# Softmax over 16,384 rows: which rows a partition holds

## The chip, the core and the metric

The kernel runs on one core of a Trainium2 chip. The core has compute engines of its own: VectorE (DVE in the profile), ScalarE (ACT), GpSimd (POOL) and TensorE (PE, unused here), and SyncE (SP), which issues the transfers. They work on an on-chip memory of 128 partitions. Sixteen DMA engines move data between that memory and the DRAM. The metric is device time in microseconds (us), from the start of an execution to its end; less is better.

## The reference

The input `x` is float32 of shape 16 x 1024 x 512, so 16,384 rows of 512 numbers (2 KB each, 33.55 MB in all). Each row is replaced by its softmax, and no row needs another:

```python
x_max = np.max(x, axis=-1, keepdims=True)
exp_x = np.exp(x - x_max)
return exp_x / np.sum(exp_x, axis=-1, keepdims=True)
```

## The kernel before

Every partition handles 128 rows. They are worked on in 16 groups of `GROUP = 8` rows per partition, so one group is 128 x 8 = 1,024 rows, 2 MB. `LOADS` and `STORES` (lines 20 and 21) join two groups to a transfer: eight loads L0 to L7 and eight stores S0 to S7, each of 128 partitions x 16 rows x 2 KB = 4 MB.

The buffer `ring` (line 78) has room for `RING = 12` groups, so six of the eight loads fit. L6 takes the place of S0's data and must wait until S0 has been written out; L7 waits for S1 in the same way (`before`, line 97, and the waits at line 197).

What is done with one group:

- The maxima of its rows, negated, on VectorE (`rowmax`, line 145; two groups at once for the `MM` entries).
- `exp(x - max)` in place and the sum of each row, on ScalarE, one instruction per row of each partition (`exps`, line 134), in a loop over the 16 groups.
- The reciprocal of the sums on VectorE (line 159), and the product of the rows and the reciprocals (line 161), on VectorE for ten groups and on GpSimd for six.

Order and queues: `SEQUENCE` (line 31) is the order of the work on VectorE and GpSimd, written by hand. `ORDER` (line 26) is that of the transfers after the first six loads: S0 S1 L6 L7 S2 S3 S4 S5 S6 S7. All sixteen transfers are issued by SyncE, on one queue, in the order L0 to L5 and then `ORDER`. A store is issued when both of its groups have been scaled (line 170). The first load is moved ahead of the barrier at the start of the program (`loads_at_the_head`).

Which rows of the DRAM a transfer touches is decided by `in_dram` (line 117), for loads (line 127) and stores (line 131) alike. Before the change, the rows are cut into eight blocks of 2,048, one for each load; inside a block partition p holds the 16 rows from 16p on. A transfer therefore touches one block of 4 MB without a gap, and the piece of one partition begins 32 KB behind that of the partition before it.

Of the kernel before, what the change touches and what calls it, by code (L numbers as in the profile page):

```python
# [15 lines left out]
GROUP = 8  # L16
# [3 lines left out]
LOADS = [2, 2, 2, 2, 2, 2, 2, 2]  # L20
STORES = [2, 2, 2, 2, 2, 2, 2, 2]
GROUPS = sum(LOADS)
LOAD_AT = [sum(LOADS[:k]) for k in range(len(LOADS))]
# [37 lines left out]
def kernel(  # L61
# [7 lines left out]
    P = nc.NUM_PARTITIONS  # L69

    x_rows, out_rows = x.flatten_outer_dims(), out.flatten_outer_dims()
    d = x_rows.shape[1]
# [17 lines left out]
    def load_of(g):  # L90
        return max(k for k in range(len(LOADS)) if LOAD_AT[k] <= g)
# [23 lines left out]
        return t[:, at(g) * GROUP : (at(g) + groups) * GROUP]  # L115

    def in_dram(t, g, groups):
        k = load_of(g)
        assert load_of(g + groups - 1) == k
        part = t[P * GROUP * LOAD_AT[k] : P * GROUP * (LOAD_AT[k] + LOADS[k]), :]  # L120
        first = (g - LOAD_AT[k]) * GROUP
        part = part.rearrange("(p r) d -> p r d", p=P)
        return part[:, first : first + groups * GROUP, :]

    def load(k):
        g, n = LOAD_AT[k], LOADS[k]
        return nc.sync.dma_start(out=rows(g, n), in_=in_dram(x_rows, g, n))

    def store(k):
        g, n = STORE_AT[k], STORES[k]  # L130
        return nc.sync.dma_start(out=in_dram(out_rows, g, n), in_=rows(g, n))
# [42 lines left out]
    with tc.manual_schedule(engines={SP}):  # L174
        for k in range(min(before)):
            first = load(k).then_inc(loaded[k], 16)
# [6 lines left out]
    for work in SEQUENCE.split():  # L183
        kind = work.rstrip("0123456789")
        g = int(work[len(kind) :])
# [4 lines left out]
    for transfer in ORDER.split():  # L190
        k = int(transfer[1:])
# [39 lines left out]
```

## Time and profile before

| | |
|---|---|
| Median of 3 timed runs | 159.82 us (159.81 to 160.81) |
| The profiled execution: own time | 160.08 us |
| Its span, first to last recorded work | 158.8 us |
| VectorE busy | 121.8 us, 77% of the span, 36 instructions |
| ScalarE busy | 92.2 us, 58%, 257 instructions |
| GpSimd busy | 42.3 us, 27%, 10 instructions |
| Moved by the DMA engines | 67.11 MB in 2,304 packets, 423 GB/s over the span |
| A load, from issue to landing | median 25.9 us |
| A store, from issue to landing | median 24.0 us |

The own time is longer than the span by 1.28 us, which lie outside of the recorded work. The time of a transfer from issue to landing includes its wait in the queue behind earlier transfers, so it is not the time that moving 4 MB takes. Busy shares are averages: VectorE works from 12 us to 138 us and hardly pauses in between, while the DMA engines work from the first microsecond to the last.

### The profile page before, as it was taken

Reading aid. Unit: us, or ns where it says so; the run is one execution under the profiler, and the core shown is the slowest. Engines: PE = TensorE matmul, PEld = TensorE weight load, DVE = VectorE, ACT = ScalarE, POOL = GpSimd, SP = SyncE. Lnnn points to the kernel's source line nnn. Section 1 sums busy time; section 2 is a strip of 40 time slices with the busy share of each in tenths; the row PEclk is TensorE's granted clock in tenths of the full one; section 3 lists DMA queues with packets and bytes.
Section 4 is the critical chain, followed back from the end, with each engine's and each line's share of the span. In section 5 each row is a group of like instructions: output and inputs, shape, how many; then the busy total and the mean of one; then the engine's idle time right before and its main releaser. Section 6 shows DMA issues by size and latency. Waiting matters only on the chain.

```text
span 158.8 us, 572 instructions
## 1 busy us (share of the span) xinstructions
DVE 121.8 (77%) x36; ACT 92.2 (58%) x257; POOL 42.3 (27%) x10
## 2 busy tenths in 40 slices
DVE  0008979999999999999999499999999999700000
ACT  0300699969406999999988990899599300000000
POOL 0000000000007903930970790079049300000000
DMA  7999999999999999999999999999999999999996
GB/s 264 438 479 405 405 495 421 396 438 471 413 405 438 471 405 396 396 413 471 438 396 462 446 413 405 454 421 438 438 421 446 413 446 438 438 421 438 429 429 264
DMA packets 2304, 67.11 MB, mean 423 GB/s; under 512 B 256, under 2 KB 256, under 8 KB 256
## 3 DMA queue, kind: packets, MB, share of 16 engines
q1 hardware_dynamic: 2304, 67.11, 98.9%
HBM read 33.55 MB, written 33.55 MB: 423 GB/s over the span
## 4 chain that ended last, share of the span: by engine, by line
DMA 45%; DVE 39%; issue 2%; DVEq 0%
DMA ring<-in_x_dram 26%; DVE ring L161 22%; DMA out_dram<-ring 20%; DVE stat L145 16%; DVE recip L159 1%; DVEq L144 0%
## 5 line engine op out<-in xcount | busy, mean ns | idle before, releaser
L134 ACT ACTIVATE ring<-ring,stat x128 | 90.4, 707 | 28.1 <-ACTq L151 28.1
L145 DVE TENSOR_REDUCE stat<-ring 128x16 f32<-128x8192 f32 (+1 forms) x10 | 69.5, 6956 | 15.7 <-DMA ring<-in_x_dram 15.7
L161 POOL TENSOR_TENSOR ring<-ring,recip 128x4096 f32<-128x4096 f32 x6 | 42.1, 7016 | 81.8 <-DVE recip L159 81.8
L161 DVE TENSOR_TENSOR ring<-ring,recip 128x4096 f32<-128x4096 f32 x10 | 51.1, 5109 | 0.3
L134 ACT ACTIVATION_READ_ACCUMULATOR ring<-ring,stat x128 | 23.8, 186 | 0.0
L181 ACT ACT_TABLE_LOAD x1 | 1.3, 1283 | 4.0 <-PEq L179 4.0
L159 DVE RECIPROCAL recip<-stat 128x8 f32<-128x8 f32 x16 | 3.0, 190 | 0.0
L215 POOL MEMSET const-float32-0.0<- 128x1 f32 x1 | 0.1, 98 | 0.2 <-issue 0.2
L215 POOL MEMSET const-bfloat16-1.0<- 128x1 bf16 x1 | 0.1, 102 | 0.0
L215 POOL MEMSET const-uint8-127<- 128x1 uint8 x1 | 0.1, 102 | 0.0
L215 POOL MEMSET const-float32-1.0<- 128x1 f32 x1 | 0.1, 98 | 0.0
## 6 DMA issues: line engine op xcount, KB each, us to landing
ring<-in_x_dram SPq DMA_DIRECT2D x8, 4096.0 KB, 25.9
out_dram<-ring SPq DMA_DIRECT2D x8, 4096.0 KB, 24.0
```

The lines of the kernel that those rows point to most:

```text
L134: return nc.scalar.activation(out=row, in_=row, func=EXP, bias=one, scale=1.0, accum_out=one)
L145: nc.vector.reduce_max(out=cols(stat, g, groups), in_=rows(g, groups), axis=AX, negate=True).then_inc(maxima, groups)
L159: nc.vector.reciprocal(out=cols(recip, g), in_=cols(stat, g)).then_inc(inverted, 1)
L161: engine.tensor_mul(out=rows(g), in0=rows(g), in1=spread(cols(recip, g))).then_inc(scaled[store_of(g)], 1)
L181: nc.scalar.preload_act_table(EXP)
L215: nc = _bacc.Bacc("TRN2", target_bir_lowering=False, num_devices=1)
```

## The change

Only `in_dram` changes. The whole tensor is now split over the partitions at once: partition p holds the 128 rows from 128p on, one piece of 256 KB. Transfer k takes rows 16k to 16k + 15 of each partition's piece. A transfer still moves 128 pieces of 32 KB, but the pieces begin 256 KB apart in the DRAM, with gaps that the other seven transfers fill. Input and output are cut in the same way.

```diff
     def in_dram(t, g, groups):
-        k = load_of(g)
-        assert load_of(g + groups - 1) == k
-        part = t[P * GROUP * LOAD_AT[k] : P * GROUP * (LOAD_AT[k] + LOADS[k]), :]
-        first = (g - LOAD_AT[k]) * GROUP
-        part = part.rearrange("(p r) d -> p r d", p=P)
-        return part[:, first : first + groups * GROUP, :]
+        assert load_of(g + groups - 1) == load_of(g)
+        part = t.rearrange("(p r) d -> p r d", p=P)
+        return part[:, g * GROUP : (g + groups) * GROUP, :]
```

The buffers on the chip, the order of the sixteen transfers, the waits and every compute instruction are as before. In both built programs each transfer is one instruction over 128 x 8192 numbers; on the DRAM side the step from one partition to the next is 8,192 numbers before and 65,536 after, and the start of the second transfer is number 1,048,576 before and 8,192 after.

## The prediction

> **What bounds the kernel.** I first read the page's busy slices and its DMA lines, since the change touches nothing but transfers. The rows of digits are the busy tenths of 40 slices of the span (4 us each):
>
> ```profile
> DVE  0008979999999999999999499999999999700000
> ACT  0300699969406999999988990899599300000000
> ...
> DMA  7999999999999999999999999999999999999996
> ...
> DMA packets 2304, 67.11 MB, mean 423 GB/s; under 512 B 256, under 2 KB 256, under 8 KB 256
> ## 3 DMA queue, kind: packets, MB, share of 16 engines
> q1 hardware_dynamic: 2304, 67.11, 98.9%
> ```
>
> The DMA row has no gap from end to end, and packets occupy 98.9% of the sixteen engines' span. VectorE is nearly full in the middle but has nothing to do in the last five slices, which belong to stores alone. The packet line also tells the size of a piece: 256 of the 2,304 packets are tiny (16 transfers x 16 engines, the completion signals), so 2,048 carry data, 16 transfers x 128 partitions, and 67.11 MB / 2,048 is 32,768 bytes. One packet is already one partition's 16 rows.
>
> Then the chain that ended last:
>
> ```profile
> DMA 45%; DVE 39%; issue 2%; DVEq 0%
> DMA ring<-in_x_dram 26%; DVE ring L161 22%; DMA out_dram<-ring 20%; DVE stat L145 16%; DVE recip L159 1%; DVEq L144 0%
> ```
>
> It gives VectorE 39%, but this is one thread followed back through the waits; a store issued long before its turn makes VectorE look critical. Whether the DMA engines ever lacked work decides, so I cut the span into stretches, one for each transfer as they land (12.3 us for the first, then about every 9.7 us). Columns: the stretch and its length, busy time of VectorE, ScalarE and GpSimd, TensorE's clock (unused here), DMA share, GB/s.
>
> ```profile
> 0.00:11.90 11.90, 0.00 (x0) 1.28 (x1) 0.20 (x4) 1.00 0.97 394
> 11.90:21.60 9.70, 8.74 (x2) 4.46 (x13) 0.00 (x0) 1.00 1.00 432
> ...
> 41.00:50.70 9.70, 9.70 (x3) 2.29 (x7) 1.98 (x1) 1.00 1.00 432
> 50.70:61.00 10.30, 10.27 (x3) 10.30 (x31) 5.04 (x1) 1.00 1.00 404
> 61.00:70.70 9.70, 9.67 (x5) 9.70 (x28) 7.02 (x1) 1.00 1.00 432
> ...
> 80.40:90.10 9.70, 7.91 (x4) 8.54 (x25) 3.48 (x2) 1.00 1.00 432
> 90.10:100.10 10.00, 9.37 (x3) 5.68 (x17) 5.34 (x1) 1.00 0.99 419
> ...
> 138.90:148.60 9.70, 0.00 (x0) 0.00 (x0) 0.00 (x0) 1.00 1.00 432
> ```
>
> This table carries the prediction. A transfer takes 9.70 us at a DMA share of 1.00 and 432 GB/s, and that holds for a load on an otherwise empty chip (11.9 to 21.6), a store under a full VectorE (61.0 to 70.7) and a store with all engines idle (138.9 to 148.6). Reading the DRAM and writing it go at the same pace to the last digit. I read that as the pace of the sixteen DMA engines themselves, 1.21 us for a piece of 32 KB (9.70 us for the eight pieces of each engine), with the DRAM able to give and take more. Two stretches are slower with the engines still occupied: 10.30 us (404 GB/s) and 10.00 us (419 GB/s). In these something other than the engines' pace held the packets up, for 0.6 and 0.3 us.
>
> The profiled time adds up: the first landing at 12.3 us, fifteen more transfers x 9.70 = 145.5, the two hold-ups 0.9, together 158.7 against a span of 158.8; with the 1.28 us outside the span, 160.08 us. The median of the three runs shown, 159.82, is 0.26 us less, so the profiled run is an ordinary one and I sum against it.
>
> **The change, part by part.**
>
> *Compute and waits: 0 us.* The built program after has the same instructions on every engine in the same order, with the same shapes and waits; only line numbers and DRAM addresses differ. Rows are independent, and the same partition and columns receive other rows of the same kind. So VectorE's 121.8, ScalarE's 92.2 and GpSimd's 42.3 us stay. Their cover is the DMA stream anyway; if that slows down, VectorE waits longer for loads and the six GpSimd products have more room, so nothing there adds to it. The other direction is small too: a faster stream would meet VectorE, whose last store is issued at 137.8 us, 11 us ahead of its turn.
>
> *Number, size and order of the packets: 0 us.* Sixteen instructions on SyncE's queue as before, 128 pieces of 32 KB each, as in the program before. L6 and L7 still wait for S0 and S1. Issuing is no cost either: the sixteen issue instructions take 0.33 to 0.52 us each, and all but the first run while an earlier transfer is still being moved.
>
> *The step between pieces, 32 KB before and 256 KB after: the one unknown.* No packet of this trace steps by 256 KB, so I bound its cost from both sides.
>
> - Below nothing: the most a friendlier spread could give back is what the stream loses today. The two hold-ups are 0.9 us. The first transfer lands at 12.3 us where the chain has it begin at 0.8 us and the engines' pace needs 9.7, so 1.8 us are start-up; part of it is latency that no layout removes. Everything together is -2.7 us, 157.4 us.
> - Above: the nearest rows of a stream held up while its engines are occupied are the two stretches above. At 0.3 us per transfer, 16 x 0.3 - 0.9 = +3.9 us, 164.0 us; at 0.6 us, 16 x 0.6 - 0.9 = +8.7 us, 168.8 us. The far end is the start-up's 1.8 us paid by each of the other fifteen, 15 x 1.8 - 0.9 = +26.1 us, 186.2 us; but transfers queued behind one another show none of it today.
> - The value I take: 0 us. Twelve of the sixteen stretches lie at 429 to 439 GB/s, for reads and writes alike (the last reads 378 because a packet is counted where it starts, which also gives neighbours shares over 1.00), and a stream that is bound by its engines doesn't notice a somewhat slower DRAM until that falls below 432 GB/s. This row is the nearest one because everything else about a packet, its 32 KB in one piece above all, is unchanged.
>
> A rule of the Trainium skill speaks against the change: the page "DMA: Bandwidth & Descriptors", section "Latency and other measured facts", lists copies whose partitions lie a large power of two apart in the DRAM as slower, 207 GB/s per direction at 512 KB, 164 at 2 MB, 103 at 4 MB, against a full rate of 214. By that page's smallest step the sum would be an estimate of 160.08 x 214/207 = 165.5 us, and 256 KB is below that step, so the loss should be smaller or nothing. The trace shows no such step, so it neither agrees nor disagrees; the page calls its explanation unverified.
>
> **The rivals.** A measurement of this kernel tells differences of about 1%, 1.6 us, from no change.
>
> 1. *Forecast: nothing changes*, 159.3 to 161.4 us. For it: the equal pace of loads and stores, and 98.9% occupancy by packets that stay what they are.
> 2. *The engines meet in the DRAM (slower).* All sixteen DMA engines run at one pace, so at any moment they are at about the same place within their pieces. With pieces 256 KB apart, more low address bits are the same in all of them at once, 18 in place of 15. If those bits choose the part of the DRAM that serves a request, all sixteen queue at the same few parts. It decides from the point at which the DRAM gives less than 432 GB/s; from there a transfer takes longer than 9.70 us, and every such microsecond is on the path, since nothing covers the stream. For it: the first stretch, in which all engines begin at once, is the slowest row (394 GB/s, though start latency is in it), and the 404 stretch shows that packets can be held up. Against it: today's engines also agree in their low bits, 15 of them, at full pace. Price: 164.0 us at 419 GB/s, 168.8 us at 404 GB/s. The page named above gives 165.5 us as an estimate for twice this step, between the two.
> 3. *Faster*: the wider step spreads the requests better and the hold-ups and the start-up shrink. All of it is 157.4 us, the hold-ups alone 159.2 us. To pass 1% below, most of the start-up must go as well, and nothing ties that to the step.
> 4. *The change doesn't do what it says*: if a 32 KB piece were cut into 2 KB rows, there would be 32,768 data packets. The built program has one run of 8,192 numbers per partition in both kernels, so I give it no more than 1 in 100, inside the slower side.
>
> **How the numbers follow.** Forecast 0.57. Rival 2: 0.39, of which 0.26 up to 165.5 us (the smaller of its two prices and a little above) and 0.13 beyond, 168.8 us and more. Rival 3 past 1%: 0.03; rival 4: 0.01. So faster 0.03, within 1% 0.57, slower 0.40. The predicted time is the forecast's: the sum against the profiled run is 160.08 and against the median 159.82, and I say 160.0 us. The range goes from 159.2 us (the hold-ups gone) to 165.5 us, which leaves out about 0.14 above, with rival 4, and 0.04 below.
>
> **What would show it.** In the profile after: the same 2,304 packets, none more between 512 B and 8 KB; stretches of 9.70 us per transfer at 432 GB/s with VectorE, ScalarE and GpSimd at 121.8, 92.2 and 42.3 us. Rival 2 would show as stretches of 10 us and more at 419 GB/s or less with the DMA share still near 1.00, in loads before 61 us, in stores after it, or in both. It would make the prediction wrong, and which of the two directions pays would tell where the DRAM is narrow. Rival 3 would show as an earlier first landing and no 404 stretch.

## The result, and the profile after

The changed kernel takes 160.79 us (median of 7 runs, 160.55 to 161.81), the kernel before 159.84 us (median of 7 runs, 159.76 to 160.81). The ratio is 1.0062, with a 95% interval of 1.0034 to 1.0090: slower by 0.95 us. The interval leaves out no change at all, so the loss is real; it is also within the 1% that the prediction called no change.

The profiled execution after took 160.94 us with a span of 159.6 us (before: 160.08 and 158.8). The page of after, in the parts that were read before:

```profile
DVE  0008979999999999999999299999999999600000
...
DMA  7999999999999998999999999999999999999994
...
DMA packets 2304, 67.11 MB, mean 420 GB/s; under 512 B 256, under 2 KB 256, under 8 KB 256
## 3 DMA queue, kind: packets, MB, share of 16 engines
q1 hardware_dynamic: 2304, 67.11, 98.7%
...
DMA 45%; DVE 39%; issue 2%; DVEq 0%
```

The packets are the same in number and size, the chain has the same shares, and VectorE, ScalarE and GpSimd are busy for 121.8, 92.3 and 42.3 us. The stream has no gap either; only the mean rate fell, from 423 to 420 GB/s. So the transfers themselves became slower somewhere. The stretches of after, one for each transfer as it lands (columns as before: the stretch, its length, busy times of VectorE, ScalarE and GpSimd, TensorE's clock, DMA share, GB/s):

```profile
0.00:11.90 11.90, 0.00 (x0) 1.28 (x1) 0.20 (x4) 1.00 0.96 394
11.90:21.60 9.70, 8.75 (x2) 4.46 (x13) 0.00 (x0) 1.00 1.00 432
41.00:50.70 9.70, 9.70 (x3) 2.29 (x7) 1.97 (x1) 1.00 1.00 432
50.70:61.70 11.00, 10.97 (x4) 11.00 (x33) 5.05 (x1) 1.00 0.98 381
61.70:71.40 9.70, 9.67 (x5) 9.70 (x28) 7.02 (x1) 1.00 1.00 432
...
90.80:101.10 10.30, 9.75 (x3) 5.36 (x17) 4.64 (x1) 1.00 1.02 426
101.10:110.80 9.70, 9.70 (x3) 9.70 (x28) 6.04 (x1) 1.00 0.99 429
139.80:149.50 9.70, 0.00 (x0) 0.00 (x0) 0.00 (x0) 1.00 1.00 432
```

With steps of 256 KB a transfer still takes 9.70 us at 432 GB/s, the early loads and the stores alike. Two stretches are longer than before, and they are the two that were already slow: 11.0 us where it was 10.3, and 10.3 where it was 10.0. Both belong to a load that has a store behind it in the queue: L5 before S0, and L7 before S2.

The chain of work in order of time (start, length, what) shows the same shift, first in the kernel before:

```profile
39.96 31.10 DMA out_dram<-ring
71.07 0.02 issue
71.08 19.52 DMA ring<-in_x_dram
```

and then in the kernel after:

```profile
39.97 31.78 DMA out_dram<-ring
71.75 0.02 issue
71.77 19.46 DMA ring<-in_x_dram
```

S0 is issued at the same moment, 39.96 and 39.97 us, behind L5 in the queue, and lands 0.68 us later. What follows it, S1 and L6, takes no longer than before.

The trace records when each transfer lands. From the landing of L4 to that of L7, five transfers (L5, S0, S1, L6, L7) took 49.29 us before and 50.29 us after; five times 9.70 is 48.5. So the loss against the engines' pace grew from 0.79 to 1.79 us here, while from L7's landing to the last store's both kernels need the same (58.28 and 58.13 us). All of the difference is in this part, nearly all of it in L5 (10.17 us from landing to landing before, 10.84 after) and L7 (9.85 and 10.23). These are one execution of each kernel. In both, the slow pieces are the last two that each DMA engine moves of L5: the very last ones take 1.79 us on average before and 2.09 us after, in place of 1.21, and the pieces of S0 behind them take 1.21 us again.

### The profile page after: what moved, and what is told of

Same layout as the page of the kernel before. It is cut to its first block, busy times and chain, and to the rows that moved or that the text cites. A ratio compares the mean times of both kernels' runs of the same rounds, so it can differ in the third digit from the quotient of the medians.

```text
span 159.6 us, 572 instructions
## 1 busy us (share of the span) xinstructions
DVE 121.8 (76%) x36; ACT 92.3 (58%) x257; POOL 42.3 (26%) x10
## 4 chain that ended last, share of the span: by engine, by line
DMA 45%; DVE 39%; issue 2%; DVEq 0%
DMA ring<-in_x_dram 26%; DVE ring L158 22%; DMA out_dram<-ring 20%; DVE stat L142 16%; DVE recip L156 1%; DVEq L141 0%
```

## The experiments

### One side at a time

The first question was which of the two directions pays. Two kernels keep the step of one side at 32 KB; `in_block` and `in_whole` are the two versions of `in_dram`. The first:

```diff
-        return nc.sync.dma_start(out=rows(g, n), in_=in_dram(x_rows, g, n))
+        return nc.sync.dma_start(out=rows(g, n), in_=in_whole(x_rows, g, n))
...
-        return nc.sync.dma_start(out=in_dram(out_rows, g, n), in_=rows(g, n))
+        return nc.sync.dma_start(out=in_block(out_rows, g, n), in_=rows(g, n))
```

> Only the eight loads step by 256 KB, the eight stores by 32 KB as before; the rows of the output come out in another order than the reference's, all the work is done. In the trace of after, what it lost against before lies in two stretches, each the last load ahead of a store: L5 before S0 (landing 10.84 us after the one before it, 10.17 before the change) and L7 before S2 (10.23 against 9.85). Theory A (the slow load is slow for the step at which it reads): the whole loss is here, 160.8 us, L5 at about 10.8 us. Rival B (the stores that follow are what holds it up, by the step at which they write): as before, 159.8 us, L5 at about 10.2 us. Rival C (both sides in part): between, 160.3 us.

Measured: 160.72 us, ratio 1.0052 (1.0031 to 1.0072) against the kernel before, whose median in this comparison was 159.90 us. L5 landed 11.41 us after L4 in the profiled execution, more than in after, and L7 9.92 us after L6, less than in after: single executions share the loss out differently, so the medians decide.

The second has `in_block` and `in_whole` exchanged.

> Only the eight stores step by 256 KB, the loads by 32 KB; again the rows of the output come out in another order. Theory A (step of the loads): as before, 159.8 us, L5 at about 10.2 us. Rival B (step of the stores): 160.8 us, L5 at about 10.8 us. Rival C: 160.3 us.

Measured: 160.19 us, ratio 1.0008 (0.9992 to 1.0025); L5 after 10.32 us. The step of the loads carries nearly the whole loss; that of the stores is too small to be told from nothing here. This speaks for theory A, and against B.

### More changes from a load to a store

If the loss belongs to a load that has a store behind it, more of these should cost more. In this order L5, L6 and L7 each stand between two stores, so that L4, L5, L6 and L7 are followed by a store, four in place of two. Everything is computed as before.

```diff
-S0 S1 L6 L7 S2 S3 S4 S5 S6 S7
+S0 L5 S1 L6 S2 L7 S3 S4 S5 S6 S7
...
-        for k in range(min(before)):
+        for k in range(5):
...
-            last = before[k]
-            since = max([a for a in awaited if a < last], default=-1)
-            nc.sync.wait_ge(stored[last], 16 * (last - since))
+            if k in before:
+                last = before[k]
+                since = max([a for a in awaited if a < last], default=-1)
+                nc.sync.wait_ge(stored[last], 16 * (last - since))
```

> The layout of before, with L5, L6 and L7 each put between two stores (L0 to L4, S0 L5 S1 L6 S2 L7 S3 and so on), so that a store follows a load four times instead of twice. Theory S (the hold-up belongs to the change from a load to a store): four slow loads of about 0.15 to 0.6 us each, L4, L5, L6 and L7, 160.4 to 161.0 us. Rival T (the hold-up belongs to what the engines do at 57 and 98 us, or to the two loads themselves): two hold-ups as before, 159.8 us.

Measured: 160.53 us, ratio 1.0049 (1.0020 to 1.0078). The slow packets moved with the order: those at 57 to 59 us and at 98 us are gone, and new ones begin at 47 to 50, 69, 88 to 90 and 108 to 110 us, at the ends of L4, L5, L6 and L7. One row, 11 us that hold L4 (432 GB/s in the same place of the order of before, where no store follows L4):

```profile
41.00:52.00 11.00, 11.00 (x3) 3.60 (x11) 3.37 (x1) 1.00 0.97 381
```

The hold-up belongs to the change, as theory S has it, and not to a time or a row. Its sizes are not those of theory S, though: L4 took 10.65 us, L5 9.70, L6 9.92 and L7 10.00, so the first change costs 0.95 us here and the others 0 to 0.3. Now the same with the layout of after:

> The layout of after with the same order as the run with four changes from a load to a store and steps of 32 KB. Theory S together with a price of the step per change: twice the difference between after and before, so about 1.9 us above the run with 32 KB, 162.3 to 162.9 us. Rival T: the difference stays 1.0 us, 160.8 us. If the wide step cost something in every load instead, the difference would stay 1.0 us too.

Measured: 162.50 us, ratio 1.0163 (1.0133 to 1.0192). The wide step now costs 162.50 - 160.53 = 1.97 us, about twice the 0.95 us that it costs with two changes: on average 0.48 to 0.49 us for each change, in either order. The intervals are too wide for so close an agreement to mean much. Had the step a price in every load, the difference would have stayed at 0.95 us and the time at 161.5 us; all six runs lie above that, at 162.02 to 163.09.

### Without the compute engines

VectorE, ScalarE and GpSimd work in the same on-chip memory while the transfers run. To see whether they have a part in it, two kernels leave all compute out and only copy.

```diff
-        nc.sync.wait_ge(scaled[k], STORES[k])
+        nc.sync.wait_ge(loaded[k], 16)
         store(k).then_inc(done_by(k), 16)
...
-    nc.scalar.preload_act_table(EXP)
-    exps()
-    for work in SEQUENCE.split():
-...
```

> The layout of before; all maxima, exponentials and products are left out, each store waits for its load, so the kernel only copies the input through the chip in the same sixteen transfers and in the same order. Theory D (the hold-up is between the transfers themselves, a store that begins while the last pieces of a load are under way): both hold-ups stay, L5 lands about 10.2 us after L4, and the time is 159.8 us. Rival E (the compute engines' work on the same on-chip memory holds the transfers up): L5 after 9.7 us, 158.9 us.

> The same copy without compute, with steps of 256 KB. Theory D: the difference against the copy with 32 KB stays about 1.0 us, 160.8 us, L5 about 10.8 us after L4. Rival E: no difference, 158.9 us.

Measured: 159.91 us with 32 KB (ratio 1.0001, 0.9992 to 1.0011, to the kernel before) and 160.87 us with 256 KB (1.0075, 1.0046 to 1.0105). The copy takes as long as the whole softmax, so no compute is on the path in either layout, and the difference is 0.96 us with idle engines too. L5 landed 10.25 us after L4 with 32 KB and 11.15 us with 256 KB, L7 9.71 and 10.46 us after L6; so with 32 KB the second hold-up, which theory D expected to stay, is not seen in this execution. One row each, 11 us at the end of L5, first of the copy with 32 KB (without VectorE and ScalarE the columns are GpSimd's busy time, clock, DMA share, GB/s):

```profile
51.00:62.00 11.00, 0.00 (x0) 1.00 1.01 405
```

and of the copy with 256 KB:

```profile
51.00:62.00 11.00, 0.00 (x0) 1.00 1.01 381
```

The DMA engines are occupied throughout in both, and move 405 and 381 GB/s in place of 432. Rival E is out.

### No store while a load is under way

Is the load slow because a store begins behind it, or would its last pieces be slow anyway? Here S0 and S2 are issued only once the load ahead of them has landed.

```diff
+        if k in (0, 2):
+            nc.sync.wait_ge(loaded[5 if k == 0 else 7], 16)
         nc.sync.wait_ge(scaled[k], STORES[k])
```

> The layout of after; S0 is issued only when L5 has landed and S2 only when L7 has, so that no store begins while the pieces of a load are under way. The DMA engines stand idle at both places for issue and first bytes, about 1.5 to 2 us each. Theory D (the overlap of load and store makes the load slow): the last pieces of L5 and L7 go at the usual 1.21 us, L5 lands 9.7 us after L4; the time is 160.8 - 1.7 for the hold-ups + 3 to 4 for the gaps, 162.1 to 163.1 us. Rival F (the last pieces of a row of loads are slow by themselves, whatever follows): L5 still takes 10.8 us, 163.8 to 164.8 us.

Measured: 163.28 us, ratio 1.0209 (1.0194 to 1.0223), just above the sum that theory D gave and below the range of F. The times at which SyncE issues its transfers in this kernel:

```profile
60.78 1.25 SPq L128 DMA_DIRECT2D out_dram<-ring  x2
71.93 11.07 SPq L124 DMA_DIRECT2D ring<-in_x_dram  x2
102.06 37.85 SPq L128 DMA_DIRECT2D out_dram<-ring  x6
```

S0 leaves at 60.78 us, when L5 has landed, and L5 needed 9.69 us after L4 (10.84 in after): with nothing behind it, the load with the wide step goes at full pace. Its last packets took the usual 1.21 us, where in after they took 1.8 to 2.3 us. The price is the idle time: S0 lands 11.1 us after its issue, 1.4 us over the engines' 9.70. S1 is slow here, 10.73 us, with L6 behind it. After their pause the sixteen engines begin their pieces within 0.17 us of one another, where in after they are 1.01 us apart at this point; whether that makes S1 slow was not tested. That raised the question whether the step also matters at a change from a store to a load. The kernel before with the same added wait answers it:

> The layout of before; S0 is issued only when L5 has landed and S2 only when L7 has. With steps of 256 KB this gave 163.28 us, L5 9.70 us after L4, and S1 and L6 then slow by about 1 us at 80 to 83 us. Theory D together with A (the step matters only while a store begins behind a load): the same time within 0.3 us, 163.0 to 163.4 us, L5 again after 9.7 us, and the slow place at 80 us too. Rival J (the step has a price at the change from a store to a load as well): less slow at 80 us and 162.3 to 162.7 us.

Measured: 163.17 us, ratio 1.0200 (1.0168 to 1.0232). L5 after 9.71 us, S1 again after 10.72 us. The two layouts, 0.95 us apart in the original order, are 0.11 us apart here. So the price of the step is nearly gone once no load has a store behind it, and the slow place at 80 us is there with either step. Rival J is out.

### A step of 128 KB

Two blocks of 8,192 rows in place of one, 64 rows of a partition in one piece, in the order with four changes:

```diff
-        part = t.rearrange("(p r) d -> p r d", p=P)
-        return part[:, g * GROUP : (g + groups) * GROUP, :]
+        half = GROUPS // 2
+        part = t[P * GROUP * half * (g // half) : P * GROUP * half * (g // half + 1), :]
+        part = part.rearrange("(p r) d -> p r d", p=P)
+        return part[:, g % half * GROUP : (g % half + groups) * GROUP, :]
```

> The order with four changes from a load to a store, steps of 128 KB (two blocks of 8,192 rows, 64 rows of a partition in one piece); the same order gave 160.5 us with 32 KB and 162.5 us with 256 KB. Theory G (the price grows with the step): about half of the 2.0 us, 161.2 to 161.9 us. Rival H (a threshold between 128 and 256 KB): 160.5 us. Rival I (any step that leaves gaps costs the full price): 162.5 us.

Measured: 160.50 us, ratio 1.0046 (1.0029 to 1.0063), the same as with 32 KB (160.53). The three steps in this order, in one row each, 41 to 122 us, which hold the four changes. With 32 KB:

```profile
41.00:122.00 81.00, 71.39 (x21) 59.11 (x167) 35.09 (x5) 1.00 1.00 425
```

with 128 KB:

```profile
41.00:122.00 81.00, 71.53 (x21) 59.20 (x169) 35.08 (x5) 1.00 1.00 426
```

and with 256 KB:

```profile
41.00:122.00 81.00, 70.07 (x21) 57.74 (x164) 35.08 (x5) 1.00 1.00 418
```

From L3's landing to L7's the loss against seven times 9.70 us is 1.70, 1.58 and 3.04 us. In these single executions 256 KB costs 1.34 us more than 32 KB, less than the 1.97 us between the medians. Gaps between the pieces alone cost nothing that these runs can tell; the price begins above 128 KB, which is rival H. Whether it begins at an edge or rises steeply, two steps can't show. Theory G, by which half the step costs half, was wrong.

### One side at a time, with four changes

The difference of one side was small in the original order, so both were run again in the order with four changes.

> The order with four changes from a load to a store; loads step by 256 KB, stores by 32 KB, so the rows of the output come out in another order. The same order gave 160.5 us with 32 KB and 162.5 us with 256 KB on both sides. Theory A (the price of the step is paid by the loads that are under way when a store begins): 162.1 to 162.5 us. Rival C (both sides take part): about 161.5 us. Rival B (the stores): 160.5 us.

> The same order; stores step by 256 KB, loads by 32 KB, again with the rows of the output in another order. Theory A: 160.5 to 160.9 us. Rival C: about 161.5 us. Rival B: 162.5 us.

Measured: loads alone 161.96 us, ratio 1.0126 (1.0093 to 1.0159); stores alone 161.08 us, 1.0072 (1.0036 to 1.0109). Above the 160.53 us with 32 KB that is 1.43 us for the loads and 0.55 us for the stores, 1.98 together, against 1.97 for both at once. Theory A expected 162.1 to 162.5 us for the loads alone and 160.5 to 160.9 us for the stores alone; both medians miss it, on the side of rival C, by which both sides take part. But the interval of the stores alone overlaps that of the run with 32 KB (up to 1.0078), and two of its eight runs, at 162.4 and 162.6 us, lie apart from the other six (160.8 to 161.6), so a part of the stores in the price is likely and not settled. That the loads pay is settled: 1.0093 is above 1.0078. That they pay more than the stores is shown in the original order alone, where the intervals are apart (1.0031 to 1.0072 for the loads, 0.9992 to 1.0025 for the stores); here those of the two sides overlap.

## Why the prediction was right, and which term it missed

**The bound was right.** The DMA stream sets the time, and compute is not on the path: without any compute the kernel takes 159.91 us, as long as with it. The chain's 39% for VectorE was rightly set aside.

**Compute, waits, packets: 0 us, right.** Busy times moved by 0.1 us at most, packets and sizes are the same, and the waits follow the stream.

**The step between pieces: 0 us taken, +0.95 us measured.** This is the one term that was mis-sized. The reason given for zero holds where it was looked at: a stream of loads, or one of stores, stays at 9.70 us and 432 GB/s with steps of 256 KB. The flaw is that this row was taken to stand for all sixteen transfers. The two slow stretches were read as hold-ups by "something other than the engines' pace" and used only as prices; their place was not read. Both are loads with a store behind them, the only two such places in the order. That is where another limit than the engines' pace shows, and a change in the DRAM addresses had to be priced there: two changes at about 0.48 us.

**What was luck.** The loss stayed within 1% because this order has two such changes. With four, the same step cost 1.97 us, more than the 1.6 us that the prediction takes for no change, and its sum would again have had 0 for the step.

**Rival 2** had the right cause of a loss, the step, in the wrong place. It let every transfer fall below 432 GB/s, at 164.0 to 168.8 us, and no steady stretch did. The bounds held, since 160.79 lies between nothing and +3.9 us. Its sign, a load of 10 us and more at 419 GB/s or less with the engines occupied, is there in L5 (381 GB/s), but it was there before the change too (404 GB/s), so by itself it told nothing. Its mechanism, engines that meet because they are at about the same place within their pieces, is not borne out. In the loads of after they begin their pieces up to 0.7 us apart, more than half of 1.21. And where they were within 0.17 us, in S0 of the two kernels with the added wait, the wide step cost nothing: pieces of 1.21 to 1.28 us with either step. That was a store; loads in step were not tried.

**Rival 3** is not seen: the first landing is at 12.35 us (12.34 before) and the hold-ups grew. **Rival 4** is out by the packet line.

**The Trainium skill's rule** on rows a large power of two apart (page "DMA: Bandwidth & Descriptors", section "Latency and other measured facts") would have given an estimate of 165.5 us at twice this step and less here. This trace shows no lower rate at 256 KB in a plain stream of loads or stores; the runs agree with the page's figures only in that the larger step lost more, 128 KB nothing and 256 KB a little, and that where loads and stores meet in the queue.

**Open:** what makes the end of a load slow when a store is behind it, and why the step matters between 128 and 256 KB. That a load's reads and a store's writes then ask the DRAM for more than either alone, with the wide step lowering what it can give, is argued and not shown. The trace itself calls for caution here: the slow pieces of L5 begin from 57.3 us on, and no piece of S0 is recorded as begun before 60.7 us (60.5 before the change). So the trace shows that the store's place in the queue matters, and not the two meeting. An arrangement that keeps the step and gives the engines other addresses at the same moment was not tried.

## What to carry to other kernels

When most transfers run at the engines' pace, look at the few that don't before calling a change of addresses free: find what stands behind them in the queue, and price the change there. Here the layout cost nothing in a plain run of loads or stores, and on average half a microsecond for each load that a store follows in the queue. So keep transfers of one direction together where the buffers allow it; holding a store back until the load has landed costs more (163.3 us in place of 160.8) than leaving it queued behind.

## What the runs showed of the hardware

A change from a load to a store costs time in the engine-bound stream even with steps of 32 KB. In the original order L5 took 10.17 us for 9.70 at the first change and L7 9.85 at the second; with four changes the first took 10.65 us and the others 9.70 to 10.00. A change from a store to a load costs little in the same stream: S1 and L6 together took 19.53 us before and 19.48 after, for 19.40. After a pause, with all engines begun within 0.17 us of one another, a store with a load behind it cost 1.0 us as well (10.72 and 10.73 us), with either step. The price of the wide step came out the same on average over the changes of two orders, 0.48 and 0.49 us for each, and at 128 KB none was seen (160.50 against 160.53 us).
